# A hybrid decoder layer's tail: the second-last expert tile goes through the accumulated sum, and TensorE scales the rows in half of the final norm's blocks

## Chip, cores, metric

One core of a Trainium2 chip runs the whole layer in one launch. The metric is device time in microseconds (us), the median of several runs.

## What is computed

A layer of a decoder trunk with two attention groups, an output projection, a LayerNorm, a mixture of 32 experts (each token goes to 2 experts of one of 4 groups) and a last LayerNorm. Only the end matters here:

```python
h = layer_norm(ALPHA * h + mix, ln1_g, ln1_b)
ffn = hierarchical_moe(h, ...)        # 2 experts of one group per token
h = layer_norm(ALPHA * h + ffn, ln2_g, ln2_b)
return h[:, BLOCK:]                   # 1024 tokens x 1024, float32
```

with `layer_norm(x, g, b) = (x - mean) * rsqrt(var + eps) * g + b` per token row.

## The kernel before

The kernel is written as a list of tasks; a scheduler (`Sched.flush`) puts them in an order for each engine by estimated times, and each engine then works strictly in that order. All instructions are issued from one helper line (L312), so groups are told apart by their tiles' names.

**Expert stage.** There are 33 tiles t = 0 to 32, each of up to 128 tokens of one expert (tile 24 takes overflow). Per tile: the token rows are gathered, transposed and split in a high and a low part, multiplied with gate and up weights, put through the activation (`hidden`), transposed (`hid_tr`, whose low part is the VectorE row `hl<-tr,hh`) and multiplied with the down weights (`down`, PSUM tiles `y`, two halves of 512 columns). Consecutive tiles belong to different expert groups, so their token rows are disjoint. Tiles 0 to 30 end in `scatter`: ScalarE copies `y` to SBUF, and GpSimd issues an indirect DMA that adds the rows into `y_d`, a DRAM array of 1024 rows that already holds the residual.

**The last two tiles** (`FIX = 2`: t = 31 and 32) don't add into `y_d`. After tile 30's scatter, `old_rows` gathers their current rows from `y_d` into SBUF tiles `ZF[t]`; `down` adds `y` to them there on VectorE (`w<-y,w`, L1709). `renorm(t)` (L1806) norms these rows by themselves, scatters them to `out`, and writes `ZF[t]` back to `y_d` as well.

**The final norm** (`norm_rows`, L1787) loads the 8 blocks of 128 rows from `y_d` after tile 30's scatter, whatever tiles 31 and 32 still change. Per block: row statistics (`z_stat`: on VectorE by BN_STATS, or on ScalarE by two passes with a sum), then `z_coef` for four blocks together: a chain of small VectorE rows on `z` tiles that gives r = rsqrt(var + eps) and nm = -mean * r. Then `z_out` applies it in one of these ways:

- "A": ScalarE computes z * r + nm, VectorE multiplies by g and adds b (two 128x1024 rows `rw<-rw,rx`);
- "B": VectorE computes (z - mean) * g (row `rw<-rw,zv,rx`) and later * r + b (row `rw<-rw,z,rx`).

The blocks are `'BAAABAAA'`, statistics of blocks 2, 3, 6, 7 are on ScalarE. g and b lie broadcast over the partitions in `lnr` (tile `rx`). Each block is stored to `out` by a DMA of SyncE (SP). The indirect stores of `renorm` wait for all these stores, since they overwrite rows of tiles 31 and 32 in them. After the last of them only a check for further overflow tiles and the program's end follow.

Of the kernel before, what the change touches and what calls it, by code (L numbers as in the profile page):

```python
# [12 lines left out]
F32 = mybir.dt.float32  # L13
F32R = mybir.dt.float32r
# [3 lines left out]
AF = mybir.ActivationFunctionType  # L18
OP = mybir.AluOpType
# [4 lines left out]
D = 1024  # L24
NB = 8
# [407 lines left out]
def layer_kernel(ctx, tc, x, meta, cst, rope, lnrows, gcol, small, wr_in, w_in, w_uq, w_ukv, w_o, w_e, c_bd, c_key, c_mask, out):  # L433
    nc = tc.nc
    sched = Sched()
    sched.bias = 0.001
    V, S, G, PE, LD = (Engine(sched, n, e) for n, e in (("DVE", nc.vector), ("Activation", nc.scalar), ("Pool", nc.gpsimd),
                                                        ("PE", nc.tensor), ("SP", nc.sync)))
# [18 lines left out]
    y_d = dram.tile([NB * 128, D], F32, name="y_d")  # L457
# [19 lines left out]
    def copy_s(dst, src):  # L477
        S.activation(dst, src, AF.Copy)

    def split(hi, lo, src, eng=None):  # L480
        S.activation(hi, src, AF.Copy)
        (eng or V).tensor_tensor(lo, src, f32(hi), op=OP.subtract)
# [67 lines left out]
    ps = ap.enter_context(pool("ap", space=PSUM))  # L550
    pq4 = aw.enter_context(pool("aw", side="right"))
# [64 lines left out]
    ident = cs[:, C_ID:C_ID + 128]  # L616
# [210 lines left out]
    pb = a2.enter_context(pool("a2"))  # L827
# [450 lines left out]
    for i in range(nu + LAG + 4):  # L1278
# [9 lines left out]
        if LAG <= i < nu + LAG:  # L1288
            n, hd = units[i - LAG]
# [13 lines left out]
    idxX = keepB.tile([128, NE + 1], I32, name="idx")  # L1303
# [18 lines left out]
    OVP, FIX, NL = 24, 2, 0.0  # L1322
# [329 lines left out]
    def ix(t):  # L1652
        e = expert(t) if t != OVP and t <= NE else NE
        return slice(e, e + 1)
# [45 lines left out]
    def down(t, q):  # L1700
        hh, hl = HD[t]
        y = ps.tile([128, 512], F32, name="y", tag="y", bufs=4)
        for f in range(2):
            hi, lo = WS[t, 4 + f]
            c = slice(q * 512, (q + 1) * 512)
            mm3(y, (hh[:, f, :], hl[:, f, :]), (hi[:, c], lo[:, c]), f == 0, f == 1)
        c = slice(q * 512, (q + 1) * 512)
        if NT - FIX <= t < NT:
            V.tensor_tensor(ZF[t][:, c], y, ZF[t][:, c], op=OP.add)  # L1709
            return  # L1710
        if q == 0:
            YS[t] = pq4.tile([128, D], F32, name="w4", tag="w4", bufs=8)
        copy_s(YS[t][:, c], y)

    def scatter(t):
        own = t != OVP and t <= NE
        G.indirect_dma_start(out=View(y_d, (t - (t > OVP)) % 4, 4) if own else y_d, out_offset=Offsets(idxX[:, ix(t)]), in_=YS.pop(t), in_offset=None,
                             bounds_check=NB * 128 - 1, oob_is_err=False, compute_op=OP.add)

    def old_rows(t):  # L1720
        ZF[t] = pq4.tile([128, D], F32, name="w4", tag="w4", bufs=8)
        G.indirect_dma_start(out=ZF[t], out_offset=None, in_=y_d, in_offset=Offsets(idxX[:, ix(t)]),
                             bounds_check=NB * 128 - 1, oob_is_err=False)


    Z, ZF, ZC, STORES = ({} for _ in range(4))

    def small(name, *shape):
        return pb.tile([128] + list(shape), F32, name=name, tag=name, bufs=2)
# [7 lines left out]
    def z_stat(z, mv, on_s):  # L1737
        if on_s:
            acc = small("za", 3)
            junk = pb.tile([128, 2048], F32, name="rb", tag="rb", bufs=RB)[:, 0:D]  # L1740
            S.activation(junk, z, AF.Copy, accum_out=acc[:, 0:1])
            S.activation(acc[:, 1:2], acc[:, 0:1], AF.Copy, scale=-1.0 / D)
            S.activation(junk, z, AF.Square, bias=acc[:, 1:2], accum_out=acc[:, 2:3])
            S.activation(mv[:, 0:1], acc[:, 0:1], AF.Copy, scale=1.0 / D)
            S.activation(mv[:, 1:2], acc[:, 2:3], AF.Copy, scale=1.0 / D)
        else:
            s6 = small("zs", 2, 6)
            for q in range(2):
                ln_stats(z, s6, q)
            V.bn_aggr(mv, flat(s6))  # L1750
# [15 lines left out]
    def z_out(dst, z, m, r, nm, way, parts, store=None):  # L1766
        w = D // parts
        for q in range(parts):
            c = slice(q * w, (q + 1) * w)
            g, b = lnr[:, 0, c], lnr[:, 1, c]  # L1770
            if way == "N":
                S.activation(dst[:, c], z[:, c], AF.Identity, bias=nm, scale=r)
                V.tensor_tensor(dst[:, c], dst[:, c], g, op=OP.mult)
            elif way == "M":
                V.scalar_tensor_tensor(dst[:, c], z[:, c], m, g, op0=OP.subtract, op1=OP.mult)
                S.activation(dst[:, c], dst[:, c], AF.Copy, scale=r)
            elif way == "A":
                S.activation(dst[:, c], z[:, c], AF.Identity, bias=nm, scale=r)
                V.tensor_tensor(dst[:, c], dst[:, c], g, op=OP.mult)
                V.tensor_tensor(dst[:, c], dst[:, c], b, op=OP.add)  # L1780
            else:
                V.scalar_tensor_tensor(dst[:, c], z[:, c], m, g, op0=OP.subtract, op1=OP.mult)
                V.scalar_tensor_tensor(dst[:, c], dst[:, c], r, b, op0=OP.mult, op1=OP.add)
            if store:
                store(c)

    def norm_rows():  # L1787
        for n in range(NB):
            z_load(n)
        sched.late = NL  # L1790
        ZB = ((0, 4), (4, 8))
        for n0, n1 in ZB:
            mv = small("zv", 4, 2)
            for n in range(n0, n1):
                z_stat(Z[n], mv[:, n - n0, :], n in (2, 3, 6, 7))
            r, nm = z_coef(mv[:, 0:n1 - n0, :], n1 - n0)
            for n in range(n0, n1):
                ZC[n] = [mv[:, n - n0, 0:1]] + [a[:, n - n0:n - n0 + 1] for a in (r, nm)]
            for n in range(n0, n1):
                def store(c, n=n):  # L1800
                    LD.dma_start(out[n * 128:(n + 1) * 128, c], Z[n][:, c])
                    STORES[len(STORES)] = sched.tasks[-1]
                z_out(Z[n], Z[n], *ZC[n], 'BAAABAAA'[n], (1, 1, 1, 1, 1, 1, 1, 1)[n], store)
        sched.late = 0.0

    def renorm(t):  # L1806
        mv = small("zv", 4, 2)
        z_stat(ZF[t], mv[:, 0, :], False)
        r, nm = z_coef(mv[:, 0:1, :], 1)
        dst = pq4.tile([128, D], F32, name="w4", tag="w4", bufs=8)  # L1810
        z_out(dst, ZF[t], mv[:, 0, 0:1], r, nm, 'B', 2)
        view = (t - (t > OVP)) % 4
        G.indirect_dma_start(out=View(outs, view, 4), out_offset=Offsets(idxX[:, ix(t)]), in_=dst, in_offset=None,
                             bounds_check=NB * 128 - 1, oob_is_err=False)
        for u in STORES.values():
            sched.tasks[-1].preds[u] = u.lat
        G.indirect_dma_start(out=View(y_d, view, 4), out_offset=Offsets(idxX[:, ix(t)]), in_=ZF[t], in_offset=None,
                             bounds_check=NB * 128 - 1, oob_is_err=False)

    def overflow_table():  # L1820
        f = pb.tile([128, 7, NE], F32, name="ovf", tag="ovf", bufs=1)
# [56 lines left out]
    for t in range(NT + 1):  # L1878
        p = t - 1
        cur, nxt = t < NT, t + 1 < NT  # L1880
        if cur:
            gate_up(t, 0)
            if 0 < t < NT - 1:
                w_split(t, 5)
            if t:
                load_more()
            gate_up(t, 1)
        if nxt and t:
            w_split(t + 1, 0)
        if p >= 0:  # L1890
            hid_tr(p)
        if cur:
            gate_up(t, 2)
        if nxt:
            w_split(t + 1, 1)
            load_more()
            x_tr(t + 1, 0)
        if t == 17:
            overflow_slots()
        if cur:  # L1900
            gate_up(t, 3)
            hidden(t)
        if p >= 0:
            down(p, 0)
        if nxt:
            x_tr(t + 1, 1)
            w_split(t + 1, 2)
        if p >= 0:
            down(p, 1)
            WS.pop((p, 4)), WS.pop((p, 5))  # L1910
        if t + LEAD < NT and t:
            gather_x(t + LEAD)
        if 1 <= p < NT - FIX:
            scatter(p - 1)
        if p == NT - FIX - 1:
            scatter(p)
            for i in range(NT - FIX, NT):
                old_rows(i)
        if p >= NT - FIX:
            renorm(p)  # L1920
        if nxt:
            w_split(t + 1, 3)
            load_more()
            w_split(t + 1, 4)
        if t == NT - 2:
            w_split(t + 1, 5)
        if p == NT - FIX - 1:
            norm_rows()
        if t == 12:
            overflow_list()  # L1930
            for q in range(2):
                LD.dma_start(lnr[:, q, :], bc_row(4 + q))
        if t == 16:
            overflow_table()
# [116 lines left out]
```

## Time and profile before

| what | value |
|---|---|
| median of 3 runs | 912.03 us (911.73 to 913.14) |
| the profiled execution | 911.96 us |
| its span | 909.6 us |
| busy share PE, DVE, ACT, POOL | 88%, 75%, 56%, 34% |

PE is TensorE's matmuls, PEld its weight loads, DVE VectorE, ACT ScalarE, POOL GpSimd, SP SyncE. The span is what the trace covers; the 2.4 us beside it lie around it. The shares are means over stages: the change touches the last 60 us, where PE, at 88% over the whole span, has little to do, so the stage has to be read by itself. Times in the rows below are us from the span's start.

### The profile page before, as it was taken

The numbers are of one execution on the slowest core, as the hardware profiler recorded it, in microseconds if no ns is written. First come the engines' busy times: TensorE is split into PE (matmuls) and PEld (weight loads), VectorE is DVE, ScalarE is ACT, GpSimd is POOL, SyncE is SP. The second block draws the span as 40 slices with busy tenths as digits, with TensorE's granted clock in tenths as the row PEclk, the third lists the DMA queues.
The fourth block names the chain that finished last, engine by engine and source line by source line (L and its number), as shares of the span: only waits on it lengthen the run. The fifth ranks groups of instructions, "written<-read, shape, count | busy, mean of one in ns | idle before, by whom it ended". The sixth has DMA issues, their size and how long they took to land. (4 is left out here: it accounts for less than half of the span.)

```text
span 909.6 us, 13571 instructions
## 1 busy us (share of the span) xinstructions
PE 804.9 (88%) x4616; PEld 688.2 (76%) x4616; DVE 683.5 (75%) x1379; ACT 512.9 (56%) x966; POOL 312.9 (34%) x561
## 2 busy tenths in 40 slices
PE   3899999999999999999998499999899989998520
PEld 3898998999999988888887388888677767765410
DVE  7946623888777655658667799998897779878595
ACT  3524322576665635512122598998787768768541
POOL 3757423344331215232214324343332243332100
PEclk9999999999999999999999699999999999999855
DMA  9544512121211112799957477999999999996632
GB/s 335 175 145 169 167 67 94 46 87 55 85 50 47 48 70 70 241 354 397 348 172 281 151 264 226 349 374 363 335 343 353 321 332 366 353 347 209 197 133 104
DMA packets 49574, 196.14 MB, mean 216 GB/s; under 512 B 12689, under 2 KB 14225, under 8 KB 37345
## 3 DMA queue, kind: packets, MB, share of 16 engines
q1 hardware_dynamic: 36688, 166.41, 49.3%
q0 software_dynamic: 12816, 28.87, 11.5%
q8 instruction: 37, 0.61, 0.3%
q14 instruction: 33, 0.26, 0.1%
HBM read 165.57 MB, written 49.05 MB: 236 GB/s over the span
## 5 line engine op out<-in xcount | busy, mean ns | idle before, releaser
L312 DVE TENSOR_TENSOR wlg<-rw,whg 128x1024 fp32r<-128x1024 f32 x120 | 143.3, 1220 | 32.4 <-ACT whg L312 32.1
L312 POOL DMA_INDIRECT y_d<-w,idx x33 | 72.4, 2193 | 224.6 <-ACT w L312 180.4
L312 ACT ACTIVATE whg<-rw 128x1024 fp32r<-128x1024 f32 x120 | 124.5, 1060 | 42.5 <-DMA rw<-in_w_e_dram 37.2
L312 PE MATMUL sc<-wh,ht 128*128 128x448 f32 (+3 forms) x400 | 116.2, 371 | 1.9 <-DVE ht L312 1.3
L312 PE MATMUL gu<-wlg,xh 128*128 128x512 f32 x264 | 106.3, 403 | 10.4 <-DVE wlg L312 10.4
L312 PE MATMUL gu<-whg,xh 128*128 128x512 f32 x264 | 109.3, 414 | 2.8 <-ACT whg L312 2.8
L312 PE MATMUL gu<-whg,xl 128*128 128x512 f32 x264 | 104.9, 398 | 2.1 <-DVE xl L312 2.1
L312 PEld LDWEIGHTS sc<-wh,ht 128*128 128x128 f32 x400 | 74.3, 192 | 9.5 <-DVE ht L312 1.8
L312 PE MATMUL sc<-wl,ht 128*128 128x448 f32 (+3 forms) x200 | 73.1, 365 | 0.0
L312 PEld LDWEIGHTS gu<-wlg,xh 128*128 128x128 f32 x264 | 49.9, 189 | 28.7 <-DVE wlg L312 18.1
L312 DVE TENSOR_TENSOR wld<-rw,whd 128x1024 fp32r<-128x1024 f32 x58 | 68.3, 1220 | 2.1 <-ACT whd L312 2.1
L312 PEld LDWEIGHTS gu<-whg,xh 128*128 128x128 f32 x264 | 50.0, 190 | 13.4 <-ACT whg L312 4.8
L312 PEld LDWEIGHTS gu<-whg,xl 128*128 128x128 f32 x264 | 50.2, 190 | 12.8 <-DVE xl L312 4.0
L312 ACT ACTIVATE whd<-rw 128x1024 fp32r<-128x1024 f32 x58 | 58.3, 1059 | 0.3 <-PE y L312 0.3
L312 PE MATMUL y<-whd,hh 128*128 128x512 f32 x124 | 51.3, 414 | 0.0
L312 PE MATMUL sc<-w,oT 128*128 128x512 f32 x192 | 49.8, 402 | 0.6 <-DMA oT<-o_d 0.6
L312 PE MATMUL tr<-cs,w 128*128 128x128 f32 x264 | 40.4, 277 | 10.9 <-DMA w<-h_d,idx 7.3
L312 DVE TENSOR_TENSOR xl<-tr,xh 128x512 fp32r<-128x512 f32 x66 | 45.2, 685 | 6.4 <-ACT xh L312 6.1
L312 ACT ACTIVATE pt<-sc,ng 128x272 f32<-128x272 f32 (+9 forms) x56 | 29.8, 538 | 34.5 <-DVE ng L312 34.3
L312 PE MATMUL y<-wld,hh 128*128 128x512 f32 x124 | 49.1, 396 | 0.0
L312 PE MATMUL y<-whd,hl 128*128 128x512 f32 x124 | 49.0, 395 | 0.0
L312 POOL DMA_INDIRECT w<-h_d,idx x33 | 44.1, 1337 | 11.2 <-issue 5.5
(331 smaller groups left out, 1961.3 us busy)
## 6 DMA issues: line engine op xcount, KB each, us to landing
rw<-in_w_e_dram SPq DMA_DIRECT2D x88, 1024.0 KB, 20.7
o_d<-oT SPq DMA_DIRECT2D x16, 512.0 KB, 2.7
oT<-o_d POOLq DMA_DIRECT2D x16, 512.0 KB, 8.5
x<-in_w_in_dram SPq DMA_DIRECT2D x8, 672.0 KB, 6.3
u_d<-r SPq DMA_DIRECT2D x7, 672.0 KB, 3.3
h_d<-h SPq DMA_DIRECT2D x8, 512.0 KB, 3.2
hr<-h_d SPq DMA_DIRECT2D x8, 512.0 KB, 9.7
h_d<-hr SPq DMA_DIRECT2D x8, 512.0 KB, 4.5
```

The lines of the kernel that those rows point to most:

```text
L312: inst = getattr(t.eng.real, method)(*[self.real(a) for a in args], **{k: self.real(v) for k, v in kw.items()})
```

## The change

Tile 31 is no longer fixed up in SBUF. It is scattered into `y_d` like the others (its `y` copied by ScalarE), after the 8 block loads have read `y_d`, and its finished rows are then gathered back. Tile 32 keeps the old way. `renorm` of tile 31 uses a new way "P", and writes nothing back to `y_d`.

Way "P": VectorE computes (z - mean) * g as in "B". ScalarE makes a 128x128 diagonal matrix `dg` of r (identity scaled per row). TensorE multiplies `dg` with each 512 columns (float32), and adds b by two matmuls of one row of ones with b's high and low part (`DG["one"]`, `DG["b"]`, float32r, made once by `shift_row`). ScalarE copies the PSUM result out, and each half is stored by its own DMA. The blocks become `'BPBPAPAP'`, statistics on ScalarE are those of blocks 1, 3, 5, 7. The code that applies the norm moves to a function `norm_out`, recorded after tile 32, ahead of both `renorm`.

```diff
     def down(t, q):
...
-        if NT - FIX <= t < NT:
+        if t == NT - 1:
             V.tensor_tensor(ZF[t][:, c], y, ZF[t][:, c], op=OP.add)
             return
...
     def z_out(dst, z, m, r, nm, way, parts, store=None):
...
-            if way == "N":
+            if way == "P":
+                dg = DG.get("dg")
+                if q == 0:
+                    DG["dg"] = dg = pb.tile([128, 128], F32, name="dg", tag="dg", bufs=2)
+                    S.activation(dg, ident, AF.Copy, scale=r)
+                V.scalar_tensor_tensor(dst[:, c], z[:, c], m, g, op0=OP.subtract, op1=OP.mult)
+                for a in range(q * w, (q + 1) * w, 512):
+                    e = slice(a, a + 512)
+                    p = ps.tile([128, 512], F32, name="y", tag="y", bufs=4)
+                    PE.matmul(p, dg, dst[:, e], start=True, stop=False)
+                    for x in DG["b"]:
+                        PE.matmul(p, DG["one"], x[:, e], start=False, stop=x is DG["b"][1])
+                    copy_s(dst[:, e], p)
+                    if store:
+                        store(e)
+                continue
+            elif way == "N":
...
+    def shift_row():
+        one = pb.tile([128, 4, 128], F32R, name="xh", tag="xh", bufs=3)[0:1, 0, :]
+        V.tensor_scalar(one, iota[0:1, :], 0.0, 1.0, op0=OP.mult, op1=OP.add)
+        DG["one"], DG["b"] = one, [pq4.tile([128, D], F32R, name="w4", tag="w4", bufs=8)[0:1, :] for _ in range(2)]
+        split(DG["b"][0], DG["b"][1], lnr[0:1, 1, :])
+
     def norm_rows():
...
-                z_stat(Z[n], mv[:, n - n0, :], n in (2, 3, 6, 7))
+                z_stat(Z[n], mv[:, n - n0, :], n in (1, 3, 5, 7))
...
-                z_out(Z[n], Z[n], *ZC[n], 'BAAABAAA'[n], (1, 1, 1, 1, 1, 1, 1, 1)[n], store)
+    def norm_out():
...
+            z_out(Z[n], Z[n], *ZC[n], 'BPBPAPAP'[n], (1, 1, 1, 1, 1, 1, 1, 1)[n], store)
     def renorm(t):
...
-        z_out(dst, ZF[t], mv[:, 0, 0:1], r, nm, 'B', 2)
+        z_out(dst, ZF[t], mv[:, 0, 0:1], r, nm, *(("P", 1) if t == NT - 2 else ('B', 2)))
...
-        G.indirect_dma_start(out=View(y_d, view, 4), out_offset=Offsets(idxX[:, ix(t)]), in_=ZF[t], in_offset=None,
-                             bounds_check=NB * 128 - 1, oob_is_err=False)
+        if t == NT - 1:
+            G.indirect_dma_start(out=View(y_d, view, 4), out_offset=Offsets(idxX[:, ix(t)]), in_=ZF[t], in_offset=None,
+                                 bounds_check=NB * 128 - 1, oob_is_err=False)
     for t in range(NT + 1):
...
-            for i in range(NT - FIX, NT):
-                old_rows(i)
-        if p >= NT - FIX:
+            old_rows(NT - 1)
+        if p == NT - 2:
+            scatter(p)
+            old_rows(p)
+        if p == NT - 1:
+            norm_out()
+            renorm(p - 1)
             renorm(p)
...
         if p == NT - FIX - 1:
+            shift_row()
             norm_rows()
```

How it moves instructions, at the three places that the prediction uses.

**VectorE, at the end of tile 31.** `hl` and `hid` belong to tiles 31 and 32, `BN_STATS zs<-rw` is a block's statistics. Before, `w_9761` is tile 31's `ZF`:

```order
L312 TENSOR_TENSOR hl<-tr,hh 128x256
L312 SCALAR_TENSOR_TENSOR hid<-gu,wsl,sil 128x256
L312 TENSOR_TENSOR w_9761<-y,w_9761 128x512 x2
L312 TENSOR_TENSOR hl<-tr,hh 128x256
L312 BN_STATS zs<-rw 128x6 x3
```

With the change (`w_9783` is the low part of b's row, `w_9763` is tile 32's `ZF`):

```order
L312 TENSOR_TENSOR w_9783<-rx,w_9767 1x1024
L312 TENSOR_TENSOR hl<-tr,hh 128x256
L312 SCALAR_TENSOR_TENSOR hid<-gu,wsl,sil 128x256
L312 BN_STATS zs<-rw 128x6 x2
L312 TENSOR_TENSOR hl<-tr,hh 128x256
L312 BN_AGGR zv<-zs 128x2
L312 SCALAR_TENSOR_TENSOR rw<-rw,zv,rx 128x1024
L312 BN_STATS zs<-rw 128x6 x2
L312 TENSOR_TENSOR w_9763<-y,w_9763 128x512
```

The first row that needs gathered rows now stands behind two blocks' statistics, and it is tile 32's.

**VectorE with the change, where the read-back enters.** `w_9896` is tile 31's rows gathered back, `z_9906` is r of blocks 0 to 3, `z_9936` r of blocks 4 to 7:

```order
L312 SCALAR_TENSOR_TENSOR z_9911<-z_9911,z_9904 128x4
L312 SCALAR_TENSOR_TENSOR rw<-rw,z_9906,rx 128x1024
L312 SCALAR_TENSOR_TENSOR z_9911<-z_9911,z_9904 128x4 x2
L312 BN_STATS zs<-w_9896 128x6
L312 SCALAR_TENSOR_TENSOR z_9936<-z_9911,z_9901 128x4
L312 BN_STATS zs<-w_9896 128x6
L312 SCALAR_TENSOR_TENSOR z_9940<-zv,z_9936 128x4
L312 BN_STATS zs<-w_9763 128x6
```

r of blocks 4 to 7 is computed one row behind the first row on the read-back.

**GpSimd's queue at the end.** `w_9761` and `w_9783` before, and `w_9763` and `w_9896` with the change, are the two tiles' `ZF`; `w_9801` is tile 31's copied `y`:

```order
-L312 DMA w_9761<-y_d,idx 128x1024
-L312 DMA w_9783<-y_d,idx 128x1024
-L312 DMA y_d<-w_9761,idx 1024x1024
-L312 DMA y_d<-w_9783,idx 1024x1024
-L312 DMA out_dram<-w_9930,idx 1024x1024
-L312 DMA out_dram<-w_9967,idx 1024x1024
+L312 DMA w_9763<-y_d,idx 128x1024
+L312 DMA y_d<-w_9801,idx 1024x1024
+L312 DMA w_9896<-y_d,idx 128x1024
+L312 DMA y_d<-w_9763,idx 1024x1024
+L312 DMA out_dram<-w_9999,idx 1024x1024
+L312 DMA out_dram<-w_9956,idx 1024x1024
```

Tile 31's gather stands behind its scatter; of the two stores to `out`, tile 32's is now first and tile 31's last.

## Rows read from the trace of the kernel before

**Rows 1.** Waits, 850 to 910 us: who waited for whom, us in total, times, longest.
```profile
POOL y_d L312 <- DMA rw<-y_d: 12.2, 1, 12.2
DVE w L312 <- DMA w<-y_d,idx: 10.1, 1, 10.1
```

**Rows 2.** Windows: stretch, us, PE, PEld, DVE, ACT, POOL busy, PEclk, DMA share, GB/s.
```profile
859.00:863.00 4.00, 0.00 (x0) 0.00 (x0) 0.97 (x2) 3.23 (x7) 0.00 (x0) 0.50 1.02 403
863.00:869.00 6.00, 5.06 (x11) 3.46 (x11) 5.97 (x13) 4.97 (x15) 0.77 (x1) 0.50 0.46 186
869.00:872.60 3.60, 0.00 (x0) 0.00 (x0) 3.60 (x10) 2.76 (x8) 0.24 (x1) 0.97 0.12 38
886.00:901.00 15.00, 0.00 (x0) 0.00 (x0) 14.36 (x36) 3.50 (x3) 1.09 (x2) 0.50 0.40 158
```

**Rows 3.** Timeline of DVE: start, us, instruction, count, idle before.
```profile
862.03 1.29 DVE L312 TENSOR_TENSOR w<-y,w 128x512 f32<-128x512 f32 x2 [10.12 <-DMA w<-y_d,idx]
...
867.32 1.23 DVE L312 BATCH_NORM_STATS2 zs<-rw 128x6 f32<-128x512 f32 x2
...
875.72 1.28 DVE L312 SCALAR_TENSOR_TENSOR rw<-rw,z,rx 128x1024 f32<-128x1024 f32 x1
...
877.40 5.76 DVE L312 TENSOR_TENSOR rw<-rw,rx 128x1024 f32<-128x1024 f32 x5
...
885.93 0.16 DVE L312 SCALAR_TENSOR_TENSOR z<-z,z 128x4 f32<-128x4 f32 x1
886.01 0.15 DVE L312 TENSOR_TENSOR z<-z,z 128x1 f32<-128x1 f32 x1
...
899.20 1.41 DVE L312 SCALAR_TENSOR_TENSOR w<-w,z,rx 128x512 f32<-128x512 f32 x2
```

**Rows 4.** Timeline of POOL, same columns.
```profile
846.23 1.96 POOL L312 DMA_INDIRECT y_d<-w,idx  x1 [6.77 <-ACT w L312]
853.67 1.06 POOL L312 DMA_INDIRECT w<-y_d,idx  x1 [5.48 <-PE y L312]
...
868.23 1.01 POOL L312 DMA_INDIRECT y_d<-w,idx  x1 [12.17 <-DMA rw<-y_d]
...
899.20 0.97 POOL L312 DMA_INDIRECT out_dram<-w,idx  x1 [23.72 <-DVE z L312]
900.88 0.97 POOL L312 DMA_INDIRECT out_dram<-w,idx  x1 [0.71 <-DVEq L1942]
```

**Rows 5.** Tile `rw`, 848 to 910 us: the block loads and stores, first and last issue.
```profile
L312 SPq DMA_DIRECT2D rw<-y_d x8: 326/430/966, 852.9 to 856.9; - x8
L312 SPq DMA_DIRECT2D out_dram<-rw x8: 332/332/338, 877.0 to 895.8; - x8
```

**Rows 6.** DMA issues by narrow stretch, last number us from issue to landing: first load, last load, tile 31's gather, tile 30's scatter, the write-back at 874.47, the last store.
```profile
rw<-y_d SPq DMA_DIRECT2D x1, 512.0 KB, 3.8
...
rw<-y_d SPq DMA_DIRECT2D x1, 512.0 KB, 10.6
...
w<-y_d,idx POOLq DMA_INDIRECT x1, 8.1
...
y_d<-w,idx POOLq DMA_INDIRECT x1, 6.5
...
y_d<-w,idx POOLq DMA_INDIRECT x1, 3.1
...
out_dram<-rw SPq DMA_DIRECT2D x1, 512.0 KB, 2.6
```

**Rows 7.** Timeline of PE: the only float32 matmul of 512 columns (one instruction, two records), and tile 32's first down matmuls.
```profile
213.58 1.12 PE L312 MATMUL po<-vm,pms 64*128 64x512 f32 x2
...
864.30 1.05 PE L312 MATMUL y<-rv,hh 128*128 128x512 f32 x2
```

**Rows 8.** Timeline of ACT: four 128x128 tiles scaled by row.
```profile
214.23 1.27 ACT L312 ACTIVATE sp<-sp,sm 128x128 f32<-128x128 f32 x4
```

**Rows 9.** Page, costliest groups: copies of `y` from PSUM by ACT.
```profile
L312 ACT ACTIVATE w<-y 128x512 f32<-128x512 f32 x62 | 36.8, 594 | 10.1 <-PE y L312 10.0
```

More of the change, by code (lines that the diff above doesn't have):

```diff
@@ L1723, in old_rows @@
                              bounds_check=NB * 128 - 1, oob_is_err=False)
-    Z, ZF, ZC, STORES = ({} for _ in range(4))
+    Z, ZF, ZC, STORES, DG = ({} for _ in range(5))
     def small(name, *shape):
@@ L1798, in norm_rows, with store @@
                 ZC[n] = [mv[:, n - n0, 0:1]] + [a[:, n - n0:n - n0 + 1] for a in (r, nm)]
[L1799 to L1802, printed above, removed]
-                z_out(Z[n], Z[n], *ZC[n], 'BAAABAAA'[n], (1, 1, 1, 1, 1, 1, 1, 1)[n], store)
-        sched.late = 0.0
+        sched.late = 0.0
+    def norm_out():
+        for n in range(NB):
+            def store(c, n=n):
+                LD.dma_start(out[n * 128:(n + 1) * 128, c], Z[n][:, c])
+                STORES[len(STORES)] = sched.tasks[-1]
+            z_out(Z[n], Z[n], *ZC[n], 'BPBPAPAP'[n], (1, 1, 1, 1, 1, 1, 1, 1)[n], store)
     def renorm(t):
```

## The prediction

> **What bounds the kernel now.** The chain of waits is no help: it ends in the check after the last store. So I read the end stage backwards. In POOL's timeline the last store to `out` is issued at 900.88 [rows 4]; all that follows it (909.6 - 900.88 = 8.7 us of span, 2.4 us around it) is untouched by the change, so its shift is the result. What holds it back is DVE, which ends its last row at 899.20 + 1.41 = 900.6 [rows 3] and is busy 14.36 of the 15 us from 886 to 901 [rows 2]. DVE has no hole from 862.03 on, and that start is late: it waits 10.1 us for one thing, gathered rows [rows 1, 3]. The first block load, issued at 852.9, had landed at 852.9 + 3.8 = 856.7 [rows 5, 6], but the statistics stand behind tile 31's add, and its gather (853.67 + 8.1 = 861.8) shares the DMA with eight loads [rows 4, 6]. So two things can help: begin DVE's work earlier, and give it less. PE is idle from 869 on [rows 2]. I work against the profiled execution, 911.96; the median of the runs shown is 0.07 higher, which I neglect.
>
> **Head start.** Tile 31's two adds (1.29) go, and with them the wait. DVE starts at 856.7: statistics of block 0 (1.23), tile 32's `hl` (0.3, half of an add of 0.65), block 0's first pass (1.2: between 5.76/5 = 1.15 and 1.28), statistics of block 2 (1.23), to about 861 [rows 3]. Then comes tile 32's add, whose gather is now the first in POOL's queue: 861.8 as before, or half a microsecond later. PE's matmuls for it start behind `hl` at 858.2; twelve at 5.06/11 = 0.46 us, at the 1.2 GHz level (granted 0.50) [rows 2], end at 863.8, so both adds are done at about 864.2. After that, in the order listed: five first passes (6.0), two pairs of statistics (2.5), some 18 small rows at 0.1 (885.93 to 886.01 is 0.08) [rows 3] and two second passes (2.4), 12.7 in all: 876.9. r of blocks 0 to 3 is ready ahead of the second passes, at 874.2.
>
> **The read-back.** Tile 31's scatter waits for all block loads, as tile 31's write-back did [rows 1]: the last load landed at 856.9 + 10.6 = 867.5, POOL issued at 868.23 [rows 4 to 6]. One gather less beside the loads may give 0.2: 868.0. Tile 30's adding scatter took 6.5 to land [rows 6], on DMA engines as free as these will be: 874.5. POOL needs the same 0.7 to go on: the gather is issued at 875.2. Its price is not in the trace: the nearest rows are 3.1, the write-back at 874.47 on free engines, and 8.1, the gather beside eight loads [rows 6]. Beside it now run two 512 KB stores, not eight loads, so I take 3.8, near the low end: 879.0; with 8.1 it would be 883.3. DVE reaches it at 876.9 and waits 2.1. Behind this wait stand r of blocks 4 to 7 and so, on ACT, the way A pass of block 4 and the copies behind it. PE passes that: four `y` buffers hold blocks 1 and 3. By the Trainium skill (DMA: Bandwidth & Descriptors, "SWDGE vs HWDGE vs iDMA") each DMA engine takes the software and the hardware queues in turn, so that a few gathered rows would not wait for whole stores: 3.8, and 906.3. The trace's 8.1 beside loads does not look like turns: 8.1, and 910.4.
>
> **DVE's rest.** From 879.0: four half statistics (2.5), tile 31's first pass (1.2), way A's four rows of blocks 4 and 6 (4.6), tile 32's four halves (2.8) and 24 small rows (2.4), 13.5: DVE ends at 892.5 where it ended at 900.6. As work, four blocks and tile 31 lose a 1.2 us row each and tile 31 its adds, 7.3; the rest is the head start less the new wait. Tile 31's r is ready some 1.9 earlier, at 890.6.
>
> **PE and the stores.** Eight half blocks, then two of tile 31, in one row from 874.2 + 0.3 (`dg`, 1.27/4 [rows 8]) + 0.1 = 874.6. A half is one float32 matmul of 512 columns (1.12 at the 2.4 GHz level [rows 7]) and two float32r ones (half of 0.46 each): 1.58, and 3.16 at the low level. That row has 64 rows of weights where these have 128, and the float32r ones have a single one; time going by columns, I take neither as a difference. PE was idle before 863.7, the granted clock was 0.50, and it stood at 0.97 only from 869, after 5.06 us of work [rows 2]. I take 5.1 us at the low level here as well: 1.6 halves by 879.7, then 6.4 x 1.58 = 10.1: 889.8. ACT's copy (0.6 [rows 9]) and SP's issue give 890.5, the store lands 2.6 later [rows 6] at 893.1. The first store to `out` waits for that landing, as it did before: 895.8 + 2.6 = 898.4, issued at 899.20 [rows 4, 5]. So 893.9, and the second behind it, with 0.97 and a gap of 0.3, at 895.2. Tile 31's own path: 890.6 + 0.3 + 2 x 1.58 + 0.6 + 0.3 = 895.0. The last store moves from 900.88 to 895.2: 911.96 - 5.7 = **906.3**.
>
> The Trainium skill (FP8 and Floating Point Precision, "TensorE Precision Notes") counts four passes for a true float32 matmul; as an estimate that is 4 x 512 columns, 0.85 at 2.4 GHz, where the row has 1.12. By it the last store would go at 894.4 and the run would take 905.5. The row decides.
>
> **At no cost.** `shift_row` adds a one-partition row on ACT (about 1.0) and on DVE (1.2), ahead of `hl`. DVE waits there until 856.7 anyway; tile 31's `y` comes 1 us later, and nobody needs it before 868. Without that cover it would cost 1.2. Two more copies of `y` on ACT lie in the wait for the first load. SP issues twelve stores instead of eight, 0.3 apiece, with time between. Tile 32's write-back now stands behind the gather on POOL, at about 880; the stores behind it come 13 us later. Tile 31's write-back goes, and nobody waited for it.
>
> **Rivals.**
> - *PE stays at its low level.* For: it is at 0.50 when the blocks begin, rose in this stage only once, after 5 us of work, and had fallen back by 886 [rows 2]; and nearly a third of the new time is matmuls with one row of weights, a form not in this trace. Against: the first four halves have no wait between them. Price: eight halves at 3.16 end at 899.9, tile 31's two at 906.2, copy and issue 0.9: the last store at 907.1, **918.2**, slower by 6.2. It decides from a half of 2.5 on: 874.6 + 25.4 + 0.9 is 900.9.
> - *The read-back is late.* The gather at 8.1 lands at 883.3, DVE and all behind it move by 4.3: tile 31's path ends at 899.3, **910.4**. From 6 us of delay on the gain is gone. For: stores share the DMA, and the scatter at 6.5 is itself one row. Against: both rows beside free engines, 3.1 and 2.6, are short.
> - *PE is at its high level at once, and the read-back is in time.* Eight halves then end at 887.2, the last store of a block lands at 890.5, and tile 31's path, 2.1 earlier, ends at 892.9: 904.0. For: PE works on tile 32 until 863.8. Against: it idles 10 us from there. This is the low end.
>
> **How the numbers follow.** Forecast, between 905 and 909: 0.65. PE high at once, 903 to 905: 0.17. Late read-back, 909 to 913: 0.10, half of it under 910.2. PE low: 0.08. The range reaches from the low end, less 0.7 for what the rounded rows may add up to, to the late read-back: 903.3 to 910.4, which leaves about 0.15 out. A measurement of this kernel tells 0.2% (1.8 us) from no change. Faster: 0.65 + 0.17 + 0.05 = 0.87; same 0.05; slower 0.08.
>
> **What would show it.** In the profile after: DVE's first block statistics near 857, not 863.6; DVE's wait on the gather between 877 and 880, some 2 us long, and none over 3 elsewhere; tile 31's scatter at 868, landing in about 6.5; PE's granted clock at 0.50 when way P begins and at 1.00 some 5 us later; halves of 1.6 us then; the last store 5 to 6 us earlier than 900.88, about 1 us after the one before. It is wrong if the clock stays at 0.50 past 885, if the wait on the gather is over 5 us, or if another row than these ends last.

## The result and the profile after

The changed kernel takes 917.10 us (median; 916.81 to 918.33) where the kernel before, in the same comparison, takes 912.59: ratio 1.0058 [1.0046, 1.0070], **slower** by 0.58%, which is little, but clear of the noise. The forecast was 906.3 and its range ended at 910.4. The profiled execution took 916.93, with a span of 914.8 (before: 911.96 and 909.6).

POOL's timeline after, for [rows 4] (start, us, instruction, idle before): tile 30's scatter, tile 31's scatter and gather, the two stores to `out`.

```profile
845.32 2.10 POOL L312 DMA_INDIRECT y_d<-w,idx  x1 [6.76 <-ACT w L312]
...
866.75 1.58 POOL L312 DMA_INDIRECT y_d<-w,idx  x1 [12.66 <-ACT zv L312]
873.22 1.50 POOL L312 DMA_INDIRECT w<-y_d,idx  x1 [4.88 <-issue]
...
901.80 0.99 POOL L312 DMA_INDIRECT out_dram<-w,idx  x1 [20.40 <-issue]
906.35 0.98 POOL L312 DMA_INDIRECT out_dram<-w,idx  x1 [3.56 <-ACTq L1972]
```

The last store moved from 900.88 to 906.35, 5.5 us later; the span grew by 5.2, so that is the whole loss. (Counted from tile 30's scatter, which came 0.9 earlier in this run than in the one before, it is 6.4.) It is not DVE's doing. DVE's timeline after, for [rows 3]:

```profile
856.02 1.29 DVE L312 BATCH_NORM_STATS2 zs<-rw 128x6 f32<-128x512 f32 x2 [4.65 <-DMA rw<-y_d]
...
879.64 0.69 DVE L312 BATCH_NORM_STATS2 zs<-w 128x6 f32<-128x512 f32 x1 [4.33 <-DMA w<-y_d,idx]
...
891.31 1.41 DVE L312 SCALAR_TENSOR_TENSOR w<-w,z,rx 128x512 f32<-128x512 f32 x2
```

It begins early and ends at 892.7 instead of 900.6. The loss is on PE, which was idle here before. Its timeline, way P's first half, its last one, and tile 31's two:

```profile
872.80 2.08 PE L312 MATMUL y<-rw,dg 128*128 128x512 f32 x2 [10.73 <-ACT dg L312]
874.80 1.22 PE L312 MATMUL y<-w,xh 1*128 1x512 f32 x2
875.95 2.08 PE L312 MATMUL y<-rw,dg 128*128 128x512 f32 x2
...
896.88 1.22 PE L312 MATMUL y<-w,xh 1*128 1x512 f32 x2
899.07 2.08 PE L312 MATMUL y<-w,dg 128*128 128x512 f32 x2 [0.97 <-ACT dg L312]
901.07 1.21 PE L312 MATMUL y<-w,xh 1*128 1x512 f32 x2
902.22 2.07 PE L312 MATMUL y<-w,dg 128*128 128x512 f32 x2
904.22 1.22 PE L312 MATMUL y<-w,xh 1*128 1x512 f32 x2
```

Each half takes 3.15 us from start to start, the first (872.80 to 875.95) as the last. The windows, for [rows 2] (stretch, us, busy time of PE, PEld, DVE, ACT and POOL, PEclk, DMA share, GB/s), say why:

```profile
872.80:881.80 9.00, 9.00 (x12) 2.99 (x12) 4.64 (x12) 1.54 (x3) 2.52 (x2) 0.50 0.43 159
881.80:890.00 8.20, 8.20 (x12) 2.50 (x10) 8.20 (x18) 4.41 (x8) 0.00 (x0) 0.50 0.47 177
890.00:898.50 8.50, 8.09 (x11) 2.49 (x10) 2.58 (x14) 1.57 (x3) 0.00 (x0) 0.50 0.40 154
898.50:906.00 7.50, 6.37 (x8) 2.00 (x8) 0.00 (x0) 1.64 (x4) 0.99 (x1) 0.50 0.15 54
```

PE is busy without a break for 25 us, and the granted clock stays at 0.50, the 1.2 GHz level, to the end. The copies of tile 31's halves end the run, on ACT:

```profile
902.33 0.60 ACT L312 ACTIVATE w<-y 128x512 f32<-128x512 f32 x1 [3.31 <-PE y L312]
905.48 0.60 ACT L312 ACTIVATE w<-y 128x512 f32<-128x512 f32 x1 [2.55 <-PE y L312]
```

So the rival "PE stays at its low level" came true almost to the number (last store forecast there at 907.1, run at 918.2; way P began 1.8 earlier than forecast, and tile 31's diagonal came 1.0 behind the eighth half). What no row says yet is *why* the clock did not rise. The experiments ask that first, then what the change is worth without it.

### The profile page after: what moved, and what is told of

It reads as the page before. It is cut to its first block, busy times and chain, and to the rows that moved or that the text cites. A ratio compares the mean times of both kernels' runs of the same rounds, so it can differ in the third digit from the quotient of the medians.

```text
span 914.8 us, 13672 instructions
## 1 busy us (share of the span) xinstructions
PE 834.6 (91%) x4656; PEld 696.5 (76%) x4656; DVE 677.3 (74%) x1372; ACT 517.9 (57%) x980; POOL 312.0 (34%) x561
## 4 chain that ended last, share of the span: by engine, by line
PE 58%; DMA 16%; issue 11%; POOL 6%; DVE 6%; ACT 1%; SPq 0%; POOLq 0%; ACTq 0%; DVEq 0%
PE sc L312 32%; DMA rw<-in_w_e_dram 10%; PE tr L312 8%; PE gu L312 7%; PE y L312 6%; PE po L312 4%; DMA y_d<-w,idx 3%; POOL y_d L312 1%; POOL rsp L312 1%; DVE wlg L312 1%; DMA oT<-o_d 1%; DMA lnb<-in_lnrows_dram 1%; POOL w L312 1%; DVE h L312 1%; DMA w<-h_d,idx 1%
## 5 line engine op out<-in xcount | busy, mean ns | idle before, releaser
L312 POOL DMA_INDIRECT y_d<-w,idx x33 | 70.2, 2127 | 228.1 <-ACT w L312 175.9
L312 PEld LDWEIGHTS gu<-whg,xh 128*128 128x128 f32 x264 | 50.3, 190 | 14.2 <-ACT whg L312 5.5
L312 PEld LDWEIGHTS gu<-whg,xl 128*128 128x128 f32 x264 | 50.3, 190 | 12.7 <-DVE xl L312 3.3
L312 PE MATMUL sc<-w,oT 128*128 128x512 f32 x192 | 49.8, 402 | 0.8 <-DMA oT<-o_d 0.8
L312 ACT ACTIVATE w<-y 128x512 f32<-128x512 f32 x66 | 39.3, 595 | 17.5 <-PE y L312 17.4
```

Source lines behind the costliest of these rows:

```text
L312: inst = getattr(t.eng.real, method)(*[self.real(a) for a in args], **{k: self.real(v) for k, v in kw.items()})
```

## The experiments

Four theories on the clock: **R**, the shift's matmuls with one row of weights keep it down; **F**, the float32 matmuls do; **S**, it only has to be started; **I**, the pauses that go with one-row matmuls, not their rows. Each kernel was compared with the kernel before on its own chip. In this kernel everything up to tile 30's scatter shifts from run to run (it stood between 844.4 and 848.7 in the profiles), so the end stage is measured from that scatter to the last store to `out`: 54.7 us before (900.88 - 846.23), 61.0 after. "Half" is one half block of way P, start to start. The last two columns are of the profiled execution, which can lie some us off the median (e2_full_rows: 910.69, e4_warm: 910.96).

| kernel | us (median, or one run) | ratio to before | scatter to last store | clock in way P |
|---|---|---|---|---|
| changed kernel | 917.10 | 1.0058 [1.0046, 1.0070] | 61.0 | 0.50 |
| e1_no_shift | 907.50, one run | | 50.3 | rises |
| e2_full_rows | 908.55 | 0.9968 [0.9952, 0.9984] | 51.9 | rises |
| e3_r_diag | 912.49, one run | | 52.1 | 0.50 |
| e4_warm | 914.25 | 1.0031 [1.0013, 1.0050] | 54.8 | 1.00, falls |
| e5_sum_only | 908.82 | 0.9975 [0.9964, 0.9987] | 52.1 | (no way P) |
| e6_diag_only | 924.63, one run | | 66.8 | 0.50 |
| e7_rows_order | 906.75 | 0.9948 [0.9930, 0.9965] | 49.8 | rises |
| e8_one_shift | 905.34 | 0.9933 [0.9920, 0.9946] | 48.4 | rises |
| e9_b_31 | 903.98 | 0.9914 [0.9900, 0.9927] | 47.0 | rises |
| e10_one_buffer | 913.05, one run | | 57.5 | rises |

### What keeps the clock down

**e1_no_shift**: way P without its shift matmuls.

```diff
-PE.matmul(p, dg, dst[:, e], start=True, stop=False)
-for x in DG["b"]:
-    PE.matmul(p, DG["one"], x[:, e], start=False, stop=x is DG["b"][1])
+PE.matmul(p, dg, dst[:, e], start=True, stop=True)
```

> Way P without the two matmuls that add b (the shift is left out in blocks 1, 3, 5, 7 and in tile 31). In the changed kernel a half block took 3.16 us on PE, 2.00 of it the float32 matmul and 1.15 the two one-row ones, and the granted clock stayed at 0.50 for 33 us of unbroken work. Theory R: the one-row matmuls keep the clock down, because they fill one row of the array in 128. Then without them the clock rises to 1.00 some 4 to 7 us after way P begins (872.8), a half takes 2.0 and then 1.0 us, PE is done with the blocks by 884, and tile 31's path (r at 891.2, 0.4, 2 x 1.0, 0.9) ends the run: last store issued near 894.5 instead of 906.35, about 905 us. Theory F: the float32 matmuls keep it down. Then the clock stays at 0.50, halves take 2.0 us throughout, last store near 896.5, about 907 us. The clock decides, not the time.

Its windows around the step in the clock, way P having begun at 874.23:

```profile
874.30:878.10 3.80, 3.80 (x5) 1.72 (x6) 2.42 (x5) 0.77 (x2) 1.61 (x1) 0.50 0.50 174
878.20:888.30 10.10, 4.82 (x11) 1.74 (x10) 7.47 (x16) 5.39 (x10) 1.02 (x1) 1.00 0.58 216
```

The clock rises 3.9 us after way P begins, and stays up with PE busy 4.82 of 10.1 us. (It fell at 888.5, after waits of PE of 2.28 and 2.99 us, and was back from 895.2 on, in tile 31's matmuls.) Float32 matmuls alone do not keep it down: against F. The time is 2.5 above the forecast, 1.0 of it by the later scatter (846.35, against 845.32 in the changed kernel's profile) and 1.2 in the stage.

**e2_full_rows**: the same sum, with all 128 rows filled: the shift stands on every partition, the weights are 1/128.

```diff
-one = pb.tile([128, 4, 128], F32R, ...)[0:1, 0, :]
-V.tensor_scalar(one, iota[0:1, :], 0.0, 1.0, ...)
-... [pq4.tile([128, D], F32R, ...)[0:1, :] for _ in range(2)]
-split(DG["b"][0], DG["b"][1], lnr[0:1, 1, :])
+one = pb.tile([128, 4, 128], F32R, ...)[:, 0, :]
+V.tensor_scalar(one, iota, 0.0, 1.0 / 128, ...)
+... [pq4.tile([128, D], F32R, ...) for _ in range(2)]
+split(DG["b"][0], DG["b"][1], lnr[:, 1, :])
```

> b is added by two matmuls of 128 rows (weights 1/128, b's high and low part on all partitions) instead of one row of ones: the same sum, the same number of matmuls and columns. Theory R (one-row matmuls keep the clock down): the clock rises some 4 to 7 us after 872.8; a half takes 2.85 us at the low and 1.46 at the high level, the blocks end near 886.5, tile 31's path at 895.4; about 906 us, 11 below the changed kernel and 6 below the kernel before. Theory F (float32 matmuls keep it down): clock 0.50 throughout, halves of 2.85, last store near 902, about 913 us, as the kernel before.

Windows, then PE's timeline of a half at each level:

```profile
876.30:881.30 5.00, 5.00 (x8) 2.66 (x9) 2.44 (x5) 0.79 (x2) 1.46 (x1) 0.50 0.58 206
881.40:892.20 10.80, 8.40 (x25) 4.27 (x24) 9.08 (x18) 6.08 (x10) 1.02 (x1) 1.00 0.50 187
```

```profile
876.26 2.08 PE L312 MATMUL y<-rw,dg 128*128 128x512 f32 x2 [11.31 <-ACT dg L312]
...
878.98 1.91 PE L312 MATMUL y<-rw,dg 128*128 128x512 f32 x2
...
881.45 1.02 PE L312 MATMUL y<-rw,dg 128*128 128x512 f32 x2
...
882.77 1.02 PE L312 MATMUL y<-rw,dg 128*128 128x512 f32 x2
...
886.64 1.13 PE L312 MATMUL y<-rw,dg 128*128 128x512 f32 x2 [2.39 <-ACT dg L312]
```

With as many matmuls of as many columns and the same types, the clock rises 5.1 us after the begin; a half takes 2.72 us at the low level and 1.32 at the high one. The row count of the shift's two operands turns a loss of 0.58% into a gain of 0.32%. The forecast for R, about 906, was 2.6 too low; where the rest goes is told under "What is left once the clock rises".

**e3_r_diag**: the diagonal in float32r, the one-row shift kept.

```diff
-dg = pb.tile([128, 128], F32, ...)
+dg = pb.tile([128, 128], F32R, ...)
-V.scalar_tensor_tensor(dst[:, c], z[:, c], m, g, ...)
+dr = bw[0].tile([128, 1024], F32R, name="whg", ...)
+V.scalar_tensor_tensor(dr, z[:, c], m, g, ...)
-PE.matmul(p, dg, dst[:, e], start=True, stop=False)
+PE.matmul(p, dg, dr[:, e], start=True, stop=False)
```

> The scaling matmul in float32r (diagonal and rows rounded to it, so the low bits of these blocks are left out) beside the same one-row matmuls for b. Theory R: one-row matmuls are now 1.15 of 1.58 us of a half, the clock stays at 0.50. Theory F: no float32 matmul is left, the clock rises some 4 to 7 us after way P begins. Either way PE is no bound any more: blocks done by 886, tile 31's path decides, last store near 895.5, about 906 us.

```profile
876.00:901.00 25.00, 19.00 (x30) 7.85 (x30) 16.28 (x47) 9.61 (x17) 4.24 (x4) 0.50 0.48 179
```

No float32 matmul is left in way P, and in the window above, from its begin at 876.68 on, the clock is 0.50 throughout, also in the first four halves, 7.5 us without a break: F falls. The time was missed by 6.5 us (forecast about 906 under either theory). Of that, 3.4 is the later scatter (848.71) and 1.9 lies in the stage, since a half took 1.87 and not 1.58 us; the rest lies behind the last store.

**e4_warm**: 48 matmuls of 128 rows, whose result nobody reads, ahead of way P.

```diff
 down(p, 1)
+if p == NT - 1:
+    w = ps.tile([128, 512], F32, name="gu", tag="gu", bufs=2)
+    for _ in range(48):
+        PE.matmul(w, HD[p][0][:, 0, :], WS[p, 4][0][:, 0:512], start=True, stop=True)
```

> 48 float32r matmuls of 128x512 on old operands, result unused, fill PE's idle time between tile 32's down matmuls (862) and way P (872.8); all else as changed. The clock is then at 1.00 when way P begins. If the level only has to be reached once and unbroken work of any kind keeps it (theory S), it stays at 1.00, halves take 1.58 us and the run about 906 us. If way P's mix itself is too little for the clock (theories R and F), it falls back to 0.50 some 3 to 7 us after 872.8: 2 to 4 halves at 1.6 instead of 3.16 us, so 3 to 6 us saved at most, 911 to 914 us.

Windows, then PE's timeline of the first half:

```profile
872.60:881.60 9.00, 7.96 (x19) 2.64 (x19) 4.82 (x12) 2.72 (x5) 2.48 (x2) 1.00 0.52 192
881.80:895.00 13.20, 12.22 (x16) 3.65 (x15) 10.43 (x31) 5.05 (x10) 0.00 (x0) 0.50 0.54 205
```

```profile
872.54 1.13 PE L312 MATMUL y<-rw,dg 128*128 128x512 f32 x2 [2.41 <-ACT dg L312]
873.60 0.73 PE L312 MATMUL y<-w,xh 1*128 1x512 f32 x2
874.25 1.13 PE L312 MATMUL y<-rw,dg 128*128 128x512 f32 x2
```

Way P begins at 872.54 at 1.00, takes 1.71 per half, and loses the high level 9.2 us later with PE busy 7.96 of 9 us (one wait of 1.0 us for a diagonal in it, a smaller share than the pauses of e10_one_buffer below, and shorter than the wait of 2.39 us at 886.64 in e2_full_rows, which left the level at 1.00); then it does not come back in 12.22 us of work. S falls: the mix does not even hold the level it was given. This profile is of one of the two fastest of ten runs (910.68 to 916.63; the median of 914.25 lies just above the forecast), and the faster runs have the higher mean granted clock (0.973 at 910.68, 0.964 at 916.63). How long the level held in the slower ones no trace shows.

**e10_one_buffer**: e2_full_rows with one PSUM buffer for all of way P, so that PE must pause for ACT's copy after every half.

```diff
-p = ps.tile([128, 512], F32, name="y", tag="y", bufs=4)
+if "p" not in DG:
+    DG["p"] = ps.tile([128, 512], F32, name="y", tag="y", bufs=4)
+p = DG["p"]
```

> As e2_full_rows (shift by 128 rows), but way P uses one PSUM buffer for all its halves, so that PE waits for ACT's copy after each: a pause of about 1 us per half, 25% of the time or more, where the one-row shift only lengthened a half from 2.72 to 3.155 us (14% of it). It asks whether the pauses that go with the one-row matmuls, rather than their rows, kept the clock down. Theory R (filled rows): the granted clock still rises to 1.00 within some 4 to 8 us of way P's begin, and halves then take about 1.3 plus the pause. Rival I (array idle between matmuls): it stays at 0.50 to the end as in the changed kernel, halves 2.7 plus the pause. Time under R 912 to 916, under I 921 or more.

Windows, and a pause in PE's timeline:

```profile
871.70:875.00 3.30, 2.92 (x4) 1.17 (x4) 2.48 (x5) 0.57 (x2) 1.79 (x1) 0.50 0.41 159
...
885.30:900.50 15.20, 10.71 (x27) 4.73 (x28) 6.28 (x26) 4.71 (x9) 0.41 (x1) 1.00 0.45 172
```

```profile
887.96 1.12 PE L312 MATMUL y<-rw,dg 128*128 128x512 f32 x2 [0.69 <-ACT rw L312]
...
890.23 1.13 PE L312 MATMUL y<-rw,dg 128*128 128x512 f32 x2 [0.69 <-ACT rw L312]
```

PE pauses 0.69 us in every 2.28, is busy 10.71 of 15.2 us (70%), and holds 1.00; it had risen 3.3 us after the begin (in between PE stood still 5.2 us for a block, and it fell and rose once). The time, 913.05, is inside R's forecast. While the clock rose, PE was busy 2.92 of 3.3 us. In e4_warm the one-row shift lengthened a half at the high level from 1.32 to 1.71 us, by 23% of it, less than the 30% here, and there the level was lost. e3_r_diag was busy 76% and the changed kernel nearly all the time, both at 0.50. I falls. Of the four, R is what is left: with one row in the shift's matmuls the clock stays down or falls, with 128 it rises. One-row matmuls by themselves were not tried, so their rows and their alternation with 128-row ones are not told apart.

### What each part is worth

**e5_sum_only**: the sum and the read-back, the blocks as before.

```diff
-z_out(Z[n], Z[n], *ZC[n], 'BPBPAPAP'[n], ...)
+z_out(Z[n], Z[n], *ZC[n], 'BAAABAAA'[n], ...)
-z_stat(Z[n], mv[:, n - n0, :], n in (1, 3, 5, 7))
+z_stat(Z[n], mv[:, n - n0, :], n in (2, 3, 6, 7))
-z_out(dst, ..., *(("P", 1) if t == NT - 2 else ('B', 2)))
+z_out(dst, ..., 'B', 2)
-            shift_row()
```

> Part one alone: tile 31 goes through the sum and its rows are read back, and every block stays on DVE and ACT as before (ways BAAABAAA, statistics of 2, 3, 6, 7 on ACT, tile 31 by way B); no matmul of way P, no shift row. Theory R (the one-row matmuls alone lost the gain, the sum is sound): DVE ends where it did in the changed kernel (47.4 us behind tile 30's scatter) plus five rows of 1.2 that come back and 1.4 for tile 31, less up to 4.3 for the wait on the gather, which these rows can fill: last store 50 to 54 us behind that scatter, where the kernel before has 54.7; 907 to 911 us, same or up to 0.5% faster than before. Rival Q (reading back through the sum costs as much as the early start of DVE gives): DVE's first statistics still at 856 to 857, but a wait of 4 us or more on the gather that nothing fills, last store at 55 or later, 912 or more.

```profile
878.00:898.00 20.00, 0.00 (x0) 0.00 (x0) 19.25 (x50) 3.50 (x3) 2.25 (x3) 0.50 0.44 171
```

0.25% faster; 52.1 behind the scatter, inside the forecast. DVE has work for the time that the read-back takes and is busy 19.25 of the last 20 us: the part is sound by itself. The 0.32% of e2_full_rows is not clearly more than this (the intervals overlap): in the order that the kernel has, the diagonals add nothing that can be told from the sum alone, even where the clock rises.

**e6_diag_only**: the diagonal and the one-row shift in the kernel before (`shift_row` and way P added there, `'BPBPAPAP'`, statistics of blocks 1, 3, 5, 7 on ACT).

> Part two alone: tiles 31 and 32 are handled as in the kernel before, and the blocks are done by BPBPAPAP with the one-row shift matmuls. Theory R: the granted clock stays at 0.50 through way P although nothing of the sum is there; eight halves of 3.16 us from about 878 end at 903, the last block store lands near 907, the last store to out goes near 907.5: some 918 us, slower than before by 6 to 7. Rival Q (the read-back and its wait are what costs): without it the clock rises about 5 us after way P begins, the halves take 1.7, DVE ends at 896, and the run takes some 909.

Windows of way P (871.42 to 896.64) and of the down matmuls of tiles 31 and 32, which the order here puts behind it, then the first of each tile and DVE's wait for them:

```profile
871.50:884.00 12.50, 12.50 (x16) 3.90 (x16) 7.11 (x15) 3.45 (x7) 0.00 (x0) 0.50 0.38 147
884.00:896.60 12.60, 12.60 (x17) 3.99 (x16) 2.45 (x2) 3.80 (x6) 0.00 (x0) 0.50 0.43 166
896.70:899.80 3.10, 3.10 (x9) 2.42 (x9) 0.19 (x1) 0.60 (x1) 0.00 (x0) 0.50 0.23 85
900.00:903.70 3.70, 3.70 (x17) 2.86 (x16) 3.46 (x7) 0.00 (x0) 1.01 (x1) 1.00 0.00 0
```

```profile
896.64 0.80 PE L312 MATMUL y<-rw,hh 128*128 128x512 f32 x1
...
901.00 0.39 PE L312 MATMUL y<-rv,hh 128*128 128x512 f32 x1
```

```profile
899.61 0.69 DVE L312 TENSOR_TENSOR w<-y,w 128x512 f32<-128x512 f32 x1 [11.23 <-PE y L312]
```

The clock stays down through 25 us of unbroken way P without any part of the sum; then the same engine, still without a break, turns to 128-row matmuls and is at 1.00 some 3.3 us later. For R this is the clearest row of all. The time was missed by 6.6 us: I had left PE's order out, in which both tiles' down matmuls stand behind all eight halves, so that DVE waits 11.2 us for tile 31's.

### What is left once the clock rises

In e2_full_rows DVE still waits 4.34 us for the read-back, and PE idles behind that for diagonals (2.39 above). Behind a second such pause, of 2.51 us, the clock falls to 0.50 from 895.0 to 898.3, in tile 31's halves.

```profile
883.12 0.69 DVE L312 BATCH_NORM_STATS2 zs<-w 128x6 f32<-128x512 f32 x1 [4.34 <-DMA w<-y_d,idx]
```

Three steps on top of it:

**e7_rows_order**: the order is made as if the gather landed later.

```diff
 scatter(p)
 old_rows(p)
+sched.tasks[-1].lat = 5.0
```

> The full-rows version (128 rows of 1/128 for the shift) with one line more: the order is made as if tile 31's gather took 5 us longer to land, so that DVE has r of blocks 4 to 7 and way A's four rows ahead of its wait on the gather. Theory W (behind the clock, the next loss is the 4.3 us wait on the read-back, with r of blocks 4 to 7 behind it): the wait falls from 4.3 to under 1, PE gets its diagonals without a pause, stays at 1.00 from 5 us after way P begins up to tile 31's halves, and the last store goes about 47 us behind tile 30's scatter instead of 51.9: 903 to 905 us. Rival T (tile 31's own chain, from the gather's landing over statistics, r, diagonal, PE and copy, is what ends last and does not shorten): the last store moves by under 1.5 us, 907 to 909.

DVE's wait on the gather is gone (three of way A's rows, 880.36 to 883.9, stand ahead of it, themselves behind a wait of 1.80 for ACT) and the eight halves run in one row. But the store came 49.8 behind the scatter, not 47: PE then idles 3.72 us for tile 31's diagonal, and the clock falls back to 0.50 at 893.1. PE's timeline there:

```profile
892.02 1.13 PE L312 MATMUL y<-w,dg 128*128 128x512 f32 x2 [3.72 <-ACT dg L312]
...
893.74 1.91 PE L312 MATMUL y<-w,dg 128*128 128x512 f32 x2
```

W holds for the wait, T for what ends last; the time, 906.75, lies between the two forecasts.

**e8_one_shift**: one shift matmul instead of two; rows 0 to 63 hold the high part of the shift, the others the low part, weights 1/64.

```diff
-split(DG["b"][0], DG["b"][1], lnr[:, 1, :])
+S.activation(x, lnr[:, 1, :], AF.Copy)
+V.tensor_tensor(x[64:128, :], lnr[64:128, 1, :], f32(x[64:128, :]), op=OP.subtract)
```

> As e7_rows_order, and the two shift matmuls of a half become one: 64 rows hold the high part of the shift and 64 the low part, weights 1/64. Theory R: with 128 rows filled the clock rises as in the full-rows version; a half takes 1.09 us (0.86 + 0.23) at the high level and 2.25 at the low one. Blocks 4 to 7 are bound by ACT's copies and r rather than by PE then, so the whole gains 0.5 to 1.5 us over e7_rows_order: 902.5 to 904.5. If ACT or tile 31's chain on DVE ends last, the difference is under 0.5.

```profile
881.19 1.02 PE L312 MATMUL y<-rw,dg 128*128 128x512 f32 x2
...
882.27 1.02 PE L312 MATMUL y<-rw,dg 128*128 128x512 f32 x2
```

Halves of 1.09 us at the high level; 1.4 us better than e7_rows_order in time and in the store. The absolute forecast, which stood on that of e7_rows_order, was 0.8 too low.

**e9_b_31**: tile 31 by way B on DVE.

```diff
-z_out(dst, ..., *(("P", 1) if t == NT - 2 else ('B', 2)))
+z_out(dst, ..., 'B', 2)
```

> As e8_one_shift, with tile 31 by way B in two parts on DVE instead of way P. Theory W (tile 31's chain through the diagonal ends last: in e8_one_shift its first diagonal came 3.0 us after ACT was free, and its two halves ran at the low level up to 893.9): DVE does 1.4 us more, ending some 1.5 later, but no row follows on PE and ACT; tile 31's store goes right behind DVE's second part, the last store some 46 us behind tile 30's scatter where e8_one_shift has 48.4: 1.5 to 2.5 us faster than that, 903 to 904. Rival T (DVE's end is as late as PE's was): the last store within 0.7 of 48.4, 905 to 906.

```profile
873.40:878.80 5.40, 5.40 (x9) 2.63 (x9) 3.91 (x8) 2.69 (x5) 1.02 (x1) 0.50 0.73 271
878.90:885.00 6.10, 6.10 (x17) 2.88 (x16) 6.07 (x11) 4.34 (x8) 0.00 (x0) 1.00 0.76 285
```

```profile
891.50 1.14 POOL L312 DMA_INDIRECT out_dram<-w,idx  x1 [14.14 <-DVE z L312]
892.94 0.98 POOL L312 DMA_INDIRECT out_dram<-w,idx  x1 [0.30 <-issue]
```

The two stores now go back to back behind DVE: 903.98 us, 0.86% faster than the kernel before. The step gains 1.4 us, just under the forecast of 1.5 to 2.5; the last store goes 47.0 behind the scatter, forecast 46. This version beats both kernels, with the idea of the change kept: the sum, and half the blocks on PE. It also beats the sum alone (0.25%, intervals apart); how much of that the later place of the gather in the order would give by itself was not tried.

## Why the prediction was wrong

- **Head start**: right. DVE's first statistics at 856.02 (forecast 856.7), r of blocks 0 to 3 at 872.3 (874.2), way P at 872.80 (874.6). All times of this run lie 0.9 earlier by tile 30's scatter (845.32, against 846.23); measured from it, the first statistics are 0.2 late and way P 0.9 early.
- **The read-back**: off in size, and right in place by luck. The gather was issued 2.0 earlier than forecast (0.9 of it the earlier scatter) and was there 6.4 us later (879.64 - 873.22), not 3.8; the two nearly cancel. DVE waited 4.33, not 2.1, and went on at 879.64, forecast 879.0. What lengthened the gather was not tried. In the changed kernel this cost nothing, as PE was behind anyway; where PE is fast it does (e2_full_rows).
- **DVE's rest**: right in size, 13.1 us (879.64 to 892.7) against 13.5. That it ends at 892.7, forecast 892.5, owes as much to the luck above.
- **PE and the stores**: the step that failed, "I take 5.1 us at the low level here as well". The granted clock stayed at 0.50 through all ten halves. Eight halves at 3.15 end at 898.0, not 889.8; ACT's `dg` for tile 31, queued behind the last copy, adds 1.0, tile 31's two halves 6.3, copy and issue 1.0: 906.35. The 5.1 came from [rows 2], where PE ran matmuls with 128 rows of weights. I saw that the one-row form was not in the trace and wrote, of the price, that time goes by columns; the columns did set the price at the low level (3.16 forecast, 3.15 measured), but whether the level is reached depended on the rows, and I carried the row of one form over to another.
- **The size of a half at the high level** was off too, both ways: 1.58 forecast, 1.71 with one-row shifts (e4_warm), 1.32 with full ones (e2_full_rows). With 128 rows a float32 matmul takes 0.86 (1.32 less two at 0.23; e8_one_shift's 1.09 less 0.23 is the same) where full matmuls stand on both sides, not the 1.12 of [rows 7]. The sentence on the Trainium skill (FP8 and Floating Point Precision, "TensorE Precision Notes"), with 0.85 as an estimate, was nearer than the row that I let decide. That row had 64 rows of weights and neighbours of other forms. Which of the two made it longer is not shown: with 128 rows the first float32 matmul behind a pause is recorded with 1.13 as well (886.64 in e2_full_rows), and between one-row matmuls it takes 1.06 (872.54 to 873.60 in e4_warm).
- **At no cost**: right. DVE still waits 4.65 us for the first block load behind `shift_row`.
- **The rival** had mechanism and price, and 0.08 was too little for it: "nearly a third of the new time is matmuls with one row of weights" was the one feature without a precedent in the trace, and the argument against it, that no wait lies between the halves, was no argument on that feature. e2_full_rows, which changes the rows and nothing else on PE, shows that it decides; e6_diag_only and e3_r_diag show that neither the read-back nor the float32 matmul is needed for it.

The Trainium skill (TensorE: Matmul & The Clock Gate, "What's actually happening") has the clock set by how busy PE has been, and by sustained work it would have risen here. The traces agree for 128-row matmuls (3.3 to 6.2 us after the begin in e1, e2, e8 and e10) and disagree for the mix with one row, which PE ran unbroken for 25 us. The measurement decides.

## What to carry to other kernels

Adding a row to PSUM by a matmul with a single row of weights is cheap in columns, but here, between 128-row matmuls, it held the whole engine at half speed; filling all rows and dividing the weights by their number takes the same number of matmuls, and with them the clock rose. A part that only stops a loss should also be weighed against leaving it out: the sum alone (e5_sum_only) was, within the noise, as good as the sum with full rows. A price that hangs on the clock should be taken from a stretch of the same form of matmul; where the trace has none, both levels are full cases of the forecast, not a rival of 0.08. And when work moves to an idle engine, look at what that engine has queued behind it (both tiles' down matmuls in e6_diag_only; ACT's copies, behind which tile 31's `dg` stood) before counting the time it frees elsewhere.

## What the runs showed of the hardware that was not expected

- The granted clock stayed at 0.50 through 25 us of unbroken PE work in which two of three matmuls had one row of weights, and a level of 1.00 was lost 9.2 us into such work; with 128-row matmuls only, 1.00 was held through pauses in 30% of the time (e10_one_buffer). Row counts between 1 and 128 were not tried, nor one-row matmuls alone, nor what about the rows it is: that stays open.
- Mixing one-row and 128-row weights also lengthens a half by itself, 2.72 to 3.15 us at the low level and 1.32 to 1.71 at the high one. In the waits of the changed kernel the weight loads (PEld) stand still for "issue", in which the profile names nobody that they wait for, 19.6 us in all; in e2_full_rows, with as many matmuls, part of them at the high level, 6.7:

```profile
PEld y L312 <- issue: 19.6, 17, 1.5
```

```profile
PEld y L312 <- issue: 6.7, 20, 0.5
```
